# The moving operands of a four-layer encoder's products, moved to a pool with another byte offset

## The chip, the cores and the metric

The kernel runs on 1 core of one Trainium2 chip. The metric is the device time of one execution in microseconds (us), the median of the runs shown. Before the change it is 2073.7 us, the median of 3 runs (2072.6 to 2074.67).

## The reference

The input x has 256 tokens of 1024 features, in fp32. Four layers follow each other. Each is a gated feed-forward block (FFN), a mixer, and a second FFN, all with a residual connection and an RMS norm ahead of them:

```
for i in range(4):
    x = x + 0.5 * swiglu(rms_norm(x, norms[i, 0]), ffn_w_in[i, 0], ffn_w_out[i, 0])
    hn = rms_norm(x, norms[i, 1])
    y = (short_conv, hyena, gated_deltanet, short_conv)[i](hn)
    x = x + y
    x = x + 0.5 * swiglu(rms_norm(x, norms[i, 2]), ffn_w_in[i, 1], ffn_w_out[i, 1])
return rms_norm(x, final_norm)

def swiglu(x, w_in, w_out):          # w_in 1024 x 5632, w_out 2816 x 1024
    g, u = split(x @ w_in, 2)
    return (silu(g) * u) @ w_out
```

The short convolution projects x to 3 x 1024 features, multiplies two of the parts, convolves them over 3 tokens and gates and projects back. Hyena does the same with a long convolution by a Fourier transform, and the gated delta net is a linear attention with 8 heads. Nearly all arithmetic is in the products with the weights, some 350 MB of fp32 that are read once.

## The kernel before

**Layout of the work.** Activations lie with features on the partitions and the 256 tokens along the free axis; a tile of 128 features is 128x256. The weights are cut on the host into 665 *parts* of 128x1024 fp32, in the order in which they are used: a "c" part holds 128 output columns of a weight for all eight contraction tiles side by side, an "r" part holds 128 rows. A loop over phases (12 of them: FFN, mixer, FFN for each layer) asks for one part after the other.

**Split products.** TensorE takes the operands as float32r, and each fp32 operand is split into a high and a low half. `cut_part` (lines 263 to 285) does it for a weight part: ScalarE (ACT) copies `raw` to `wh` (L279), VectorE (DVE) subtracts to get `wl` (L281). `split_x` (L336) does it for the normalized x (`xh`, `xl`), `split` (L449) for the gated tiles that enter an output product (`hh`, `hl`). Every product of a 128x128 weight slice with a 128x256 activation tile is then three matmuls in `mm3` (L322 to L326): high weight by high activation (L324), low weight by high activation (L325), high weight by low activation (L326). The weight slice is the stationary operand, which an LDWEIGHTS puts into the array before each matmul (the profile shows it as PEld), and the activation tile is the moving operand, 256 columns of 4 bytes.

A part thus stands for 8 x 3 = 24 matmuls. In an FFN, `g` is the PSUM bank of the projection (moving operands `xh` and `xl`) and `accf` the four banks of the output product (moving operands `hh` and `hl`). `c`, `b` and `accs` are the same in the short convolution, `xv`, `x` and `acch` in hyena, `p` and `accd` in the gated delta net. In hyena `vf` and `vi` are the two halves of the Fourier transform, also by `mm3`: in `vf` a table (`th`, `tl`) is stationary and the turned values `vth`, `vtl` are moving, in `vi` the spectra `sh`, `sl` are stationary and a table is moving.

**Order.** The instructions of each engine run in the order in which the program issues them. SyncE (SP) issues the loads of `raw`, two parts (1 MB) each, into two buffers. `wh` and `wl` have rings of five parts, so the cuts on ACT and DVE run up to five parts ahead of TensorE.

**Where the tiles lie.** A pool of tiles takes a stretch of every partition; inside it each tag gets its buffers one behind the other in the order in which the tags first come up, in multiples of 32 bytes, and the pools stand one behind the other in the order in which they are opened. In the program before the change the byte addresses within a partition are:

```
pool  tile                                        first byte   byte mod 512
rp    raw, 2 buffers of 8192 bytes                     30976   256
rp    wh, 5 buffers of 4096 (wl: from 67840)           47360   256
tp    sq0, then xh0, xl0, ... xh3, xl3 (2048 each)     88320   256
tp    hh, 4 buffers of 1024                           119104   320
tp    hl, 4 buffers of 1024                           123200   320
hp    th, tl: the tables of the transform             130368   320
tq    vth, vtl; sh, sl (hyena)                        181824    64
tq    hh, hl of hyena's tiles 4 to 7                  204352    64
```

A weight slice of 128 columns is 512 bytes and an activation tile 1024 bytes, so every slice of a tile has the tile's offset modulo 512. `rp` ends at byte 88320.

In hyena the last tiles of the output product are split into the pool `tq`, since line 773 reads `self.split(y, f"{ng}_{f}", None if f < 4 else tp)` with `tp = self.tq`. The gated delta net borrows the buffers of `xh` and `xl` for its states and right sides (`xtile`), when x is no longer wanted.

Of the kernel before, what the change touches and what calls it, by code (L numbers as in the profile page):

```python
# [11 lines left out]
F32 = mybir.dt.float32  # L12
F32R = mybir.dt.float32r
# [23 lines left out]

PHASES = []
# [12 lines left out]
# ---------------------------------------------------------------- layouts  # L51
# Weight parts [128, 1024]: ("c", W, c0) = columns c0..c0+127 of W, all 8
# contraction tiles side by side; ("r", W, r0) = rows r0..r0+127 of W.
def out_tiles(f, n):
    """Rows of the output product that follow the projection of tile f."""
    if f <= LAG:
        return []
    lo = 0 if f == LAG + 1 else f - LAG
    return [t for t in range(lo, f - LAG + 1) if t < n - TAIL]
# [120 lines left out]
def shape_tables():  # L180
    f = np.float32
    # masks and ones
    i = np.arange(P)
    k, s = i[:, None], i[None, :]
    msk = np.concatenate([(k > s), (k <= s), (k < s), (k >= s), (k == s), np.ones((P, P))], axis=1).astype(f)
    # positional features of the filter network, transposed
    t = np.linspace(0.0, 1.0, L, dtype=f)[:, None]
    w = (f(2.0 * math.pi) * np.arange(L, dtype=f)[:, None] / f(L)).astype(f)
    fr = np.linspace(1e-4, 15, 16, dtype=f)[None, :]
    ph = (fr * w).astype(f)  # L190
    z = np.concatenate([t, np.cos(ph), -np.sin(ph)], axis=-1).astype(f)
    zt = np.zeros((P, L), f)
    zt[:33] = z.T
    lo, hi = math.log(1e-2) / 1.5, math.log(1e-2) / 0.3
    deltas = np.linspace(lo, hi, D, dtype=f)
    dec = np.exp((-t * np.abs(deltas)[None, :]).astype(f)).astype(f)
    dec = dec.reshape(2, P, D).transpose(1, 0, 2).reshape(P, 2 * D)
    # 512-point transform of 256 samples, frequencies 0..255 and, in place of
    # the zero sine, the Nyquist one
    n = np.arange(L)  # L200
    ang = 2.0 * math.pi * ((n[:, None] * n[None, :]) % 512) / 512.0
    fwd = np.concatenate([np.cos(ang), -np.sin(ang)], axis=1)
    fwd[:, L] = (-1.0) ** n
    inv = np.concatenate([2.0 * np.cos(ang), -2.0 * np.sin(ang)], axis=0) / 512.0
    inv[0] = 1.0 / 512.0
    inv[L] = (-1.0) ** n / 512.0
    fwd = fwd.reshape(2, P, 512).transpose(1, 0, 2).reshape(P, 1024)
    inv = inv.reshape(4, P, L).transpose(1, 0, 2).reshape(P, 1024)
    return np.concatenate([msk, zt], axis=1), dec, np.stack([fwd, inv]).astype(f)
# [5 lines left out]
# ---------------------------------------------------------------- program  # L215
class Prog:
    def __init__(self, nc, tc, io, phases, pools):
        self.nc, self.tc, self.io, self.phases = nc, tc, io, phases
        self.cp, self.rp, self.tp, self.ps = pools
        self.nparts = len(part_list(phases))  # L220
        self.next_part = 0
        self.raw = {}
        self.late = set()
        self.narrow = set()
        self.held = {}
        n = 0
        for ph in phases:
            if n:
                self.late |= {n + 3, n + 4}
            if ph[0] == "gd":  # L230
                self.narrow.add(n)
            n += len(part_list([ph]))
        self.bg = []
        self.ready = []

    # ---- weight stream
    def load_group(self, lo, n):
        nc = self.nc
        t = self.rp.tile([P, GRP, D], F32, name=f"raw{lo}", tag="raw", bufs=RAW)
        if lo < 5:  # L240
            # the first parts come in small pieces
            for o in range(n):
                step = 512 if lo + o < 3 else D
                for c in range(0, D, step):
                    self.load = nc.sync.dma_start(t[:, o, c:c + step], self.io["w"][lo + o, :, c:c + step])
        else:
            self.load = nc.sync.dma_start(t[:, :n, :], self.io["w"][lo:lo + n].rearrange("n p c -> p n c"))
# [3 lines left out]
    def load_behind(self, dst, src):  # L251
        """A load that keeps its place behind the weights."""
# [33 lines left out]
    def behind(self, i, z):  # L286
        """Parts that a new phase wants late are split behind the split of x."""
# [10 lines left out]
    # ---- products: out[col, tok] (+)= part' @ x  # L298
# [10 lines left out]
    def proj_first(self, outs):  # L309
        """A phase's first products: several parts side by side, so that the  # L310
        last tiles of x are wanted late. outs: (destination, start)."""
# [19 lines left out]
    # ---- residual update, split of x*g, and 1/rms  # L331
# [4 lines left out]
    def split_x(self, m, ng):  # L336
        nc = self.nc
        ph = self.tp.tile([P, 512], F32R, name=f"xh{ng}_{m}", tag=f"xh{m}", bufs=1)
        pl = self.tp.tile([P, 512], F32R, name=f"xl{ng}_{m}", tag=f"xl{m}", bufs=1)
# [21 lines left out]
    def rstd(self, ng, squared=False):  # L361
        """1/rms of the tokens, on every partition. Two stages, each to be
        issued behind other products."""
# [28 lines left out]
    # ---- accumulation of the output product  # L392
# [16 lines left out]
    def finish(self, pend, scale, bias, nxt):  # L409
        """The last output products, bank by bank, each bank's part of the  # L410
        residual stream updated as soon as it is complete."""
# [37 lines left out]
    def split(self, src, name, pool=None):  # L449
        """High and low parts of an SBUF tile."""  # L450
        pool = pool or self.tp
# [9 lines left out]
    # ---- phases  # L461
# [37 lines left out]
    def conv3(self, out, u, w, j, on_act=True):  # L499
        """out[t] = w0 u[t-1] + w1 u[t] + w2 u[t+1] along the free axis."""  # L500
# [50 lines left out]
    # ---- hyena: filters (spectra of the two-sided filter), then the mixer  # L551
    def sine(self, out, pre, bias, freq, tag):
        """out = sin(freq * (pre + bias)), the argument brought into [-pi, pi]."""
# [16 lines left out]
    def hy_setup(self):  # L570
        """Filter network up to its last layer; the rest goes to the background."""
# [42 lines left out]
        for c in range(2):  # L614
# [3 lines left out]
            def taps(b, c=c, cs=cs, eo=eo):  # L618
# [8 lines left out]
                if b == 0:  # L627
                    nc.vector.memset(hs[1][0:1, :], 0.0)
                    # v * d_bias is the filter's tap at zero
# [34 lines left out]
    def hy(self, ng, nxt):  # L664
# [6 lines left out]
        # constants of the short convolution: b_in enters through its taps  # L671
# [13 lines left out]
        def conv(pt, j, tag, bufs):  # L685
            """short convolution of one bank: columns j[0], j[1] of 128 features"""
# [28 lines left out]
        def turn(pr):  # L715
            """the pair's gated values with tokens on partitions"""
# [98 lines left out]
    # ---- gated delta rule, chunks of 128 tokens, both directions. With A the  # L815
    # strictly triangular matrix of a chunk, columns scaled by
    # gamma = beta / |k|^2, the chunk's solution is w = gamma * (I + A)^-1 r and
    # all products use the unscaled k and q.
    def gd(self, ng, nxt):
# [33 lines left out]
        # a large negative exponent outside the triangles  # L853
# [17 lines left out]
        def gates2(ab):  # L871
# [8 lines left out]
            # log(1 + exp(x)) = max(x, 0) + 2 atanh(u / (2 + u)), u = exp(-|x|)  # L880
# [28 lines left out]
        def decay(rg, hg, b, d):  # L909
            """E[s, c] = exp(sum of g over the tokens after s up to c), 0 outside the triangle"""  # L910
# [8 lines left out]
        def weights():  # L919
            """exp of the sums of g from a token to its chunk's end or start"""  # L920
# [17 lines left out]
        def turn(srcs, name):  # L938
            """[features, tokens] of two heads -> one bank [tokens, block, head, features]"""
# [45 lines left out]
        def kk(pr):  # L985
            """B = transposed -A of both directions"""
# [5 lines left out]
        def later():  # L992
            """Pool's work that nothing waits for yet"""
# [28 lines left out]
        # -- inverses of the 32 x 32 diagonal blocks, one block per partition  # L1022
        inv = {}

        def gather():
# [16 lines left out]
            # M[c, s] and the inverse's transpose X[s, c]; the two 16 x 16 blocks of the diagonal  # L1042
# [11 lines left out]
        def corner(stage, q):  # L1054
            """lower left 16 x 16 block: the second block's inverse times M21 times the first's"""
# [24 lines left out]
        # index 0 of the pair: block rows handled first by the recursion  # L1080
# [4 lines left out]
        def level64a(b):  # L1085
            """off-diagonal 32 x 32 blocks of the inverses of the 64 x 64 ones, and
            both put in the place of the matrix itself"""
# [38 lines left out]
        # -- chunks  # L1126
        w, S, Z, R2, wd, ot = {}, {}, {}, {}, {}, {}

        def xtile(tag, name):
            return self.tp.tile([P, 4, P], F32, name=name, tag=tag, bufs=1)  # L1130

        def solve_a(hg, b, rhs):
            """first half rows, and the right side as far as the diagonal blocks go"""
# [37 lines left out]
        def state(hg, tag):  # L1171
            """the states that the second chunks start from"""
# [11 lines left out]
        def carry(hg, tag):  # L1184
            """right sides of the second chunks"""
# [12 lines left out]
        def outp(hg, b):  # L1198
# [20 lines left out]
            # 1 / rms of o, which still lacks the factor 1 / |q| / sqrt(dk)  # L1219
# [17 lines left out]
        # -- order of work: after[n] is issued behind the products of part n  # L1237
# [23 lines left out]
        def late_silu(v):  # L1261
            """no change of table between the decays"""
# [15 lines left out]
        def unpack():  # L1278
            """convolution and silu of the heads whose bank is complete"""
# [96 lines left out]
    def final_piece(self, m):  # L1376
        """Sums of squares of a pair of feature tiles, and the pair times the
        norm's weight with tokens on partitions."""
# [54 lines left out]
    # ---- whole  # L1433
    def setup(self):
# [23 lines left out]
        # the engines' clock and table come up while the first loads run  # L1458
# [7 lines left out]
    def setup_rest(self):  # L1466
        """Tables and parameters that the first products do without."""
# [58 lines left out]
def build(nc, phases):  # L1526
# [17 lines left out]
    with tile.TileContext(nc) as tc:  # L1544
        with tc.tile_pool(name="cp", bufs=1) as cp, tc.tile_pool(name="rp", bufs=1) as rp, \
                tc.tile_pool(name="tp", bufs=1) as tp, \
                tc.tile_pool(name="ps", bufs=1, space=bass.MemoryType.PSUM) as ps:
            Prog(nc, tc, io, phases, (cp, rp, tp, ps)).run()
# [24 lines left out]
```

## Time and profile before

| what | before |
|---|---|
| time, median of 3 runs | 2073.7 us (2072.6 to 2074.67) |
| the profiled execution, first to last instruction (span) | 2073.3 us |
| TensorE (PE) busy, matmuls | 2048.9 us (99%), 17234 |
| weight loads (PEld) busy | 2028.2 us (98%), 17234 |
| VectorE (DVE) busy | 1407.5 us (68%) |
| ScalarE (ACT) busy | 1014.2 us (49%) |
| GpSimd (POOL) busy | 73.8 us (4%) |
| DMA | 356.76 MB, mean 172 GB/s |

The profile has no other time of that execution than the span; between it and the median of the runs lie 0.4 us. "Busy" counts a matmul from its start to its modelled end, and matmuls overlap in the pipeline: a matmul of 256 columns stands there with about 280 ns, while the next one starts some 120 ns after it. How fast TensorE works is therefore read from the distance of the starts, in the timeline, and not from the busy share. PEclk is the granted clock of TensorE, 1.00 being 2.4 GHz and 0.50 being 1.2 GHz.

### The profile page before, as it was taken

Reading aid. Unit: us, or ns where it says so; the run is one execution under the profiler, and the core shown is the slowest. Engines: PE = TensorE matmul, PEld = TensorE weight load, DVE = VectorE, ACT = ScalarE, POOL = GpSimd, SP = SyncE. Lnnn points to the kernel's source line nnn. Section 1 sums busy time; section 2 is a strip of 40 time slices with the busy share of each in tenths; the row PEclk is TensorE's granted clock in tenths of the full one; section 3 lists DMA queues with packets and bytes.
Section 4 is the critical chain, followed back from the end, with each engine's and each line's share of the span. In section 5 each row is a group of like instructions: output and inputs, shape, how many; then the busy total and the mean of one; then the engine's idle time right before and its main releaser. Section 6 shows DMA issues by size and latency. Waiting matters only on the chain.

```text
span 2073.3 us, 40294 instructions
## 1 busy us (share of the span) xinstructions
PE 2048.9 (99%) x17234; PEld 2028.2 (98%) x17234; DVE 1407.5 (68%) x2155; ACT 1014.2 (49%) x1546; POOL 73.8 (4%) x75
## 2 busy tenths in 40 slices
PE   9999999999999999999999998999999999999998
PEld 9999999999999999999999998899999999999998
DVE  6766867666666798666766689866667666767664
ACT  6444545445444555444544476555445444545443
POOL 0000000000000110000000021000000000000000
PEclk9999999999999999999999999999999999999999
DMA  7644455555555443555555532315554555555552
GB/s 249 233 164 153 153 183 183 183 183 173 194 183 184 163 158 128 196 184 187 181 184 185 185 123 102 123 62 185 184 184 169 199 185 185 179 185 181 186 186 95
DMA packets 93990, 356.76 MB, mean 172 GB/s; under 512 B 5810, under 2 KB 7218, under 8 KB 93619
## 3 DMA queue, kind: packets, MB, share of 16 engines
q1 hardware_dynamic: 93666, 354.18, 50.1%
q8 instruction: 135, 2.21, 0.4%
q14 instruction: 45, 0.36, 0.1%
q10 hardware_dynamic: 144, 0.00, 0.0%
HBM read 353.11 MB, written 1.05 MB: 171 GB/s over the span
## 4 chain that ended last, share of the span: by engine, by line
PE 89%; DVE 7%; DMA 2%; ACT 1%; issue 1%; POOL 0%; SPq 0%; POOLq 0%; DVEq 0%; ACTq 0%
PE g L324 16%; PE g L326 16%; PE g L325 16%; PE accf L324 8%; PE accf L326 8%; PE accf L325 8%; DVE wl L281 2%; PE c L324 1%; PE c L326 1%; PE c L325 1%; DMA raw<-w 1%; PE b L325 1%; PE b L324 1%; PE b L326 1%; PE accs L324 1%
## 5 line engine op out<-in xcount | busy, mean ns | idle before, releaser
L281 DVE TENSOR_TENSOR wl<-raw,wh 128x1024 fp32r<-128x1024 f32 (+1 forms) x667 | 811.2, 1221 | 430.7 <-ACT wh L279 430.3
L279 ACT ACTIVATE wh<-raw 128x1024 fp32r<-128x1024 f32 (+1 forms) x667 | 696.1, 1051 | 670.4 <-PE g L326 476.5
L324 PE MATMUL g<-xh,wh 128*128 128x256 f32 x2816 | 799.6, 284 | 1.0 <-ACT xh L344 0.7
L326 PE MATMUL g<-xl,wh 128*128 128x256 f32 x2816 | 798.3, 283 | 0.0
L325 PE MATMUL g<-xh,wl 128*128 128x256 f32 x2816 | 797.4, 283 | 0.3 <-DVE wl L281 0.3
L324 PEld LDWEIGHTS g<-xh,wh 128*128 128x128 f32 x2816 | 540.5, 192 | 4.1 <-ACT wh L279 2.8
L325 PEld LDWEIGHTS g<-xh,wl 128*128 128x128 f32 x2816 | 539.9, 192 | 0.6 <-DVE wl L281 0.5
L326 PEld LDWEIGHTS g<-xl,wh 128*128 128x128 f32 x2816 | 539.9, 192 | 0.2 <-DVE xl L345 0.2
L324 PE MATMUL accf<-hh,wh 128*128 128x256 f32 x1408 | 394.8, 280 | 0.0
L326 PE MATMUL accf<-hl,wh 128*128 128x256 f32 x1408 | 393.0, 279 | 0.0
L325 PE MATMUL accf<-hh,wl 128*128 128x256 f32 x1408 | 392.9, 279 | 0.0
L324 PEld LDWEIGHTS accf<-hh,wh 128*128 128x128 f32 x1408 | 264.9, 188 | 1.2 <-ACT hh L454 0.8
L326 PEld LDWEIGHTS accf<-hl,wh 128*128 128x128 f32 x1408 | 264.5, 188 | 0.0
L325 PEld LDWEIGHTS accf<-hh,wl 128*128 128x128 f32 x1408 | 264.2, 188 | 0.1
L454 ACT ACTIVATE hh<-t 128x256 fp32r<-128x256 f32 x192 | 79.8, 416 | 194.0 <-DVE t L474 189.7
L471 DVE TENSOR_TENSOR t<-g,rs 128x256 f32<-128x256 f32 x176 | 74.5, 423 | 83.8 <-PE g L326 77.2
L455 DVE TENSOR_TENSOR hl<-t,hh 128x256 fp32r<-128x256 f32 x192 | 81.4, 424 | 69.8 <-ACT hh L454 69.8
L325 PE MATMUL p<-xh,wl 128*128 128x256 f32 x256 | 74.5, 291 | 8.1 <-DVE wl L281 8.1
L472 ACT ACTIVATE t<-t 128x256 f32<-128x256 f32 x176 | 71.0, 404 | 23.4 <-DVE t L471 23.2
L324 PE MATMUL p<-xh,wh 128*128 128x256 f32 x256 | 75.8, 296 | 1.4 <-ACT wh L279 1.4
L474 DVE TENSOR_TENSOR t<-t,t 128x256 f32<-128x256 f32 x176 | 73.5, 418 | 1.5 <-ACT t L472 1.4
L326 PE MATMUL p<-xl,wh 128*128 128x256 f32 x256 | 74.1, 290 | 0.0
(315 smaller groups left out, 2424.7 us busy)
## 6 DMA issues: line engine op xcount, KB each, us to landing
raw<-w SPq DMA_DIRECT2D x330, 1024.0 KB, 4.8
raw<-w SPq DMA_DIRECT2D x6, 256.0 KB, 5.4
x<-x SPq DMA_DIRECT2D x4, 256.0 KB, 4.8
raw<-w SPq DMA_DIRECT2D x2, 512.0 KB, 6.1
dec<-dec SPq DMA_DIRECT2D x1, 1024.0 KB, 7.0
traw<-dft SPq DMA_DIRECT2D x2, 512.0 KB, 6.2
out<-ob SPq DMA_DIRECT2D x4, 256.0 KB, 2.4
w<-w SPq DMA_DIRECT2D x1, 512.0 KB, 9.0
```

The lines of the kernel that those rows point to most:

```text
L279: nc.scalar.activation(hi[:, s], src[:, s], AF.Copy)
L281: nc.vector.tensor_tensor(lo[:, s], src[:, s], hi[:, s].bitcast(F32), op=ALU.subtract)
L324: mm(out, ah, bh, start=start, stop=False, skip_group_check=True)
L325: mm(out, al, bh, start=False, stop=False, skip_group_check=True)
L326: mm(out, ah, bl, start=False, stop=stop, skip_group_check=True)
L454: self.nc.scalar.activation(hh, src, AF.Copy)
L455: self.nc.vector.tensor_tensor(hl, src, hh.bitcast(F32), op=ALU.subtract)
L471: nc.vector.tensor_tensor(t1, pg[f][:, :L], self.rs, op=ALU.mult)
L472: nc.scalar.activation(t1, t1, AF.Silu)
L474: nc.vector.tensor_tensor(t2, t1, t2, op=ALU.mult)
```

## The change

A new pool `mv` is opened between `rp` and `tp`. Its first tile, `lead`, has 80 words (320 bytes) and is never written. The tiles `xh`, `xl` (2048 bytes each, eight of them) and `hh`, `hl` (1024 bytes each, four of each) are taken from `mv` instead of `tp`; so are the gated delta net's borrowed tiles of these tags. By the rule above `mv` begins at byte 88320, `xh0` at 88640, which is byte 64 of 512, the first `hh` at 105024 (64 of 512), and `mv` ends at 113216, where `tp` begins. The rings `wh` and `wl` stay where they are, at 256 of 512. Everything opened after `tp` moves up by 320 bytes: hyena's own tiles go from 64 to 384 of 512 (`vth`, `vtl`, `sh`, `sl`, and `hh`, `hl` of its tiles 4 to 7), the transform's tables from 320 to 128. No instruction is added, removed or reordered. Comments were also dropped from the source.

```diff
+LEAD = 80
...
-        self.cp, self.rp, self.tp, self.ps = pools
+        self.cp, self.rp, self.mv, self.tp, self.ps = pools
...
+        self.mv.tile([P, LEAD], F32, name="lead")
...
-        ph = self.tp.tile([P, 512], F32R, name=f"xh{ng}_{m}", tag=f"xh{m}", bufs=1)
-        pl = self.tp.tile([P, 512], F32R, name=f"xl{ng}_{m}", tag=f"xl{m}", bufs=1)
+        ph = self.mv.tile([P, 512], F32R, name=f"xh{ng}_{m}", tag=f"xh{m}", bufs=1)
+        pl = self.mv.tile([P, 512], F32R, name=f"xl{ng}_{m}", tag=f"xl{m}", bufs=1)
...
-        pool = pool or self.tp
+        pool = pool or self.mv
         hh = pool.tile([P, L], F32R, name=f"hh{name}", tag="hh", bufs=4)
         hl = pool.tile([P, L], F32R, name=f"hl{name}", tag="hl", bufs=4)
...
         def xtile(tag, name):
-            return self.tp.tile([P, 4, P], F32, name=name, tag=tag, bufs=1)
+            pool = self.tp if tag.startswith("sq") else self.mv
+            return pool.tile([P, 4, P], F32, name=name, tag=tag, bufs=1)
...
         with tc.tile_pool(name="cp", bufs=1) as cp, tc.tile_pool(name="rp", bufs=1) as rp, \
-                tc.tile_pool(name="tp", bufs=1) as tp, \
+                tc.tile_pool(name="mv", bufs=1) as mv, tc.tile_pool(name="tp", bufs=1) as tp, \
                 tc.tile_pool(name="ps", bufs=1, space=bass.MemoryType.PSUM) as ps:
-            Prog(nc, tc, io, phases, (cp, rp, tp, ps)).run()
+            Prog(nc, tc, io, phases, (cp, rp, mv, tp, ps)).run()
```

## Rows read from the trace of the kernel before

**Rows 1.** The page: busy time by engine, and the chain that ended last.
```profile
PE 2048.9 (99%) x17234; PEld 2028.2 (98%) x17234; DVE 1407.5 (68%) x2155; ACT 1014.2 (49%) x1546; POOL 73.8 (4%) x75
...
PE 89%; DVE 7%; DMA 2%; ACT 1%; issue 1%; POOL 0%; SPq 0%; POOLq 0%; DVEq 0%; ACTq 0%
```
**Rows 2.** PE's groups: line, shapes, xcount | busy us, mean ns | idle before.
```profile
L324 PE MATMUL g<-xh,wh 128*128 128x256 f32 x2816 | 799.6, 284 | 1.0 <-ACT xh L344 0.7 <-ACT wh L279 0.3
...
L325 PE MATMUL accf<-hh,wl 128*128 128x256 f32 x1408 | 392.9, 279 | 0.0
...
L325 PE MATMUL p<-xh,wl 128*128 128x256 f32 x256 | 74.5, 291 | 8.1 <-DVE wl L281 8.1
...
L325 PE MATMUL c<-xh,wl 128*128 128x256 f32 x256 | 72.4, 283 | 0.0
...
L325 PE MATMUL xv<-xh,wl 128*128 128x256 f32 x128 | 36.3, 284 | 0.2 <-DVE wl L281 0.2
L325 PE MATMUL b<-xh,wl 128*128 128x256 f32 x128 | 36.2, 283 | 0.0
...
L325 PE MATMUL accs<-hh,wl 128*128 128x256 f32 x128 | 35.7, 279 | 0.0
```
**Rows 3.** Timeline of PE in an FFN: start us, us, line, out<-in.
```profile
401.56 0.28 PE L326 MATMUL accf<-hl,wh 128*128 128x256 f32 x1
...
404.15 0.29 PE L324 MATMUL g<-xh,wh 128*128 128x256 f32 x1
404.28 0.28 PE L325 MATMUL g<-xh,wl 128*128 128x256 f32 x1
...
405.00 0.28 PE L325 MATMUL g<-xh,wl 128*128 128x256 f32 x1
...
409.80 0.28 PE L326 MATMUL g<-xl,wh 128*128 128x256 f32 x1
```
**Rows 4.** The same view at hyena's output product: tile 0; tiles 2, 3; from tile 5.
```profile
780.86 0.28 PE L324 MATMUL acch<-hh,wh 128*128 128x256 f32 x1
...
783.22 0.28 PE L326 MATMUL acch<-hl,wh 128*128 128x256 f32 x1
...
791.43 0.28 PE L326 MATMUL vf<-vtl,th 128*128 128x256 f32 x1
...
791.79 0.28 PE L326 MATMUL vf<-vtl,th 128*128 128x256 f32 x1
791.91 0.28 PE L324 MATMUL acch<-hh,wh 128*128 128x256 f32 x1
...
797.35 0.28 PE L324 MATMUL acch<-hh,wh 128*128 128x256 f32 x1
...
802.83 0.28 PE L326 MATMUL vi<-tl,sh 128*128 128x256 f32 x1
802.95 0.28 PE L324 MATMUL acch<-hh,wh 128*128 128x256 f32 x1
...
807.71 0.28 PE L324 MATMUL acch<-hh,wh 128*128 128x256 f32 x1
```
**Rows 5.** Stretches: busy us (xcount) of PE, PEld, DVE, ACT, POOL; PEclk, DMA share, GB/s.
```profile
780.80:783.20 2.40, 2.40 (x22) 2.40 (x22) 2.40 (x6) 1.14 (x2) 0.00 (x0) 1.00 0.00 0
...
791.95:797.20 5.25, 5.25 (x49) 5.25 (x48) 5.11 (x9) 2.33 (x3) 0.00 (x0) 1.00 0.62 203
```
**Rows 6.** The same view over stages: two of FFNs and short convolutions, hyena, delta net, start.
```profile
36.00:690.00 654.00, 653.97 (x5363) 644.69 (x5362) 431.68 (x628) 309.80 (x424) 9.66 (x10) 1.00 0.54 183
...
690.00:812.00 122.00, 121.69 (x1026) 121.29 (x1025) 107.47 (x183) 63.26 (x96) 18.84 (x23) 1.00 0.43 146
1179.00:1400.00 221.00, 206.28 (x1945) 196.73 (x1944) 180.85 (x363) 133.86 (x323) 28.06 (x23) 0.95 0.31 109
0.00:36.00 36.00, 33.16 (x245) 32.35 (x246) 25.60 (x44) 24.13 (x39) 3.20 (x6) 0.95 0.73 253
```
**Rows 7.** The page: DVE's cut of a weight part, its busy time, mean and idle time.
```profile
L281 DVE TENSOR_TENSOR wl<-raw,wh 128x1024 fp32r<-128x1024 f32 (+1 forms) x667 | 811.2, 1221 | 430.7 <-ACT wh L279 430.3
```

## The prediction

> **What bounds the kernel now.** The order of reading is: the page's busy times and chain, then PE's groups, then the timeline of PE, then the loads of the other engines in the same stretches. The page says that PE is busy over 99% of the span and that 89% of the chain that ended last is PE, 7% DVE [rows 1]. The groups show almost no idle time ahead of the large products: 1.0 us before 2816 matmuls of `g`, none before `accf`; the only large one is 8.1 us ahead of `p` in the delta net [rows 2]. So the span is set by the distance between the starts of successive matmuls, and that is to be read in the timeline.
>
> There it has more than one value, although every one of these matmuls has the same form (128x128 by 128x256, granted clock 1.00, that is 2.4 GHz). In `g`, 40 steps from 405.00 to 409.80 take 4.80 us: 120.0 ns. In `accf`, 22 steps from 401.56 to 404.15 take 2.59 us: 117.7 ns [rows 3]. In `acch` the first tile has 20 steps in 2.36 us, 118.0 ns; the tiles 2 and 3 have 48 steps from 791.91 to 797.35, 5.44 us, 113.3 ns; from tile 5 on it is 42 steps in 4.76 us, again 113.3 ns [rows 4].
>
> What differs? Not what the other engines do: the slow 118.0 ns was seen with the DMA engines at a share of 0.00, the fast 113.3 ns with the DMA at 0.62, DVE busy in both [rows 5]. What differs is the byte offset of the moving operand against that of the weight slice which is loaded meanwhile, by the table of addresses. The weights are at 256 of 512 in all three. `g` moves tiles at 256, `accf` and the early `acch` tiles at 320, the last four `acch` tiles at 64. The offset 256 gives 120.0, 320 gives 118 in all FFNs, 64 gives 113.3. One thing spoils the table: tiles 2 and 3 of `acch` lie at 320 and still run at 113.3. They come directly behind `vf`, whose moving operand lies at 64 [rows 4]. I read it so: load and matmul run side by side in a cycle that repeats itself, an offset can hold more than one such cycle, and the work before decides which. At 320 two are seen, at 64 against 256 only the fast one. It was reached from `vi`, which ran at 120, as in the step from 802.83 to 802.95 [rows 4], and kept to the end.
>
> **The change part by part.** It removes and adds no instruction, wait or transfer, so nothing is moved past a queue. What it may alter is the step of PE.
>
> (1) `g`, `c` and `b`: 3 x 2816, 3 x 256 and 3 x 128 matmuls (each has three such rows, of which one is shown) [rows 2], together 9600. `c` and `b` have the same mean as `g`, 283 ns, and are put at its step. Their moving operand goes from 256 to 64, the pair of the fast `acch`. If they take its step, each saves 120.0 - 113.3 = 6.7 ns: 64.3 us.
>
> (2) `accf` and `accs`: 3 x 1408 and 3 x 128, together 4608 [rows 2], from 320 to 64: 117.7 - 113.3 = 4.4 ns each, 20.3 us. With (1) this is 84.6 us, and it lies on the path wholly: in the stretch of FFNs and short convolutions PE is busy 653.97 of 654.00 us [rows 6].
>
> (3) Hyena and the delta net: `xv` and `x` (576 matmuls), `p` (768), at 6.7 ns 9.0 us; `accd` and the first half of `acch` (192 and 96) at up to 4.4 ns, 1.0 us, as half of the 96 already run fast. But here DVE is busy 107.47 of 122 us and 180.85 of 221 us [rows 6], and PE waits 8.1 us for a cut in `p`. A faster PE arrives earlier at the same waits. Bounds: nothing and 10 us. I take 3, nearer to nothing, since the DVE share of 82 to 88% leaves little to shorten.
>
> (4) The tiles 4 to 7 of hyena's output product move from 64 to 384, since they stay in `tq`. They are 96 matmuls that run at 113.3 today. No row shows 384 against 256; the bounds are 113.3 and 120.0, so 0 to 0.6 us lost. I take 0.3. The transform moves with its tables by the same 320 bytes, its two operands keep their distance; `vf` and `vi` stay at their 120: nothing. The fp32 products of the delta net, some 480 matmuls of 128 columns or fewer, shift too: at most 6.7 ns each either way, 3 us; I take nothing, as no row tells of a sign.
>
> (5) What a faster PE meets. The weights must come faster by 120/113.3, at most 1.06. In the FFNs DVE goes from 431.68 of 654, 66%, to 70%, ACT from 47% to 50%, the DMA from 183 to 194 GB/s, where the first 36 us show 253 GB/s [rows 6]. So the steady supply holds. At each of the 11 borders between phases, the new x must be updated and split before new parts are cut, and there PE comes nearest to its supply. The bounds are nothing and one cut on DVE per border, 1.22 us [rows 7], 13 us in all. I take 2, near nothing, since today PE's wait on cuts is 0.3 us in 2816 matmuls of `g` [rows 2].
>
> (6) Stores of ACT and DVE to the new places: the edit costs nothing there as long as PE covers them, with a third of DVE's time idle in the FFNs [rows 6]; without that cover a longer split would show as PE waiting for `hh` or `hl`.
>
> The sum: 84.6 + 3 - 0.3 - 2 = 85.3 us less. The profiled execution has a span of 2073.3 us, so 1988.0; the median of the runs lies 0.4 us above that span, so 1988.4, and I say 1988. What is late next: still PE, at 113.3 ns a step.
>
> Its own range: at best 84.6 + 10 + 0, about 1979; at worst 84.6 + 0 - 0.6 - 13 = 71.0, and so 2003.
>
> **The rivals.** (A) The other cycle. Since 320 holds two cycles, 64 may hold the slow one too, and the borders, with transposes and sums between the products, may start it each time. Then `g`, `c`, `b` go only to 117.7, 9600 x 2.3 = 22 us, and `accf` stays: 2052 (with mixtures in between). For it: tile 0 of `acch`, directly behind transposes, ran at 118.0. Against it: that tile lay at 320, and no matmul with 64 against 256 ran slow.
>
> (B) The offset is not the cause. Tiles 2 and 3 speak for it: same offset as `accf`, other step. Then something else at the end of hyena set the step, `g` stays at 120.0 and the time at 2074. Against it: `g` and `accf` alternate in each FFN, and the step changes with them within a few matmuls, through 128 ns from 404.15 to 404.28, to an exact 120.0 [rows 3], under the same weights, clock and engines; operand tiles and destination bank are all that is exchanged. By the Trainium skill, "TensorE: Matmul & The Clock Gate", Part 2, TensorE has two SBUF read ports, one for the moving operand and one for weight loads, and loading the next weights takes no read bandwidth from the running matmul. By that rule offsets would not meet at all, and the sum would be nothing, the time of B. The two steps of 120.0 and 117.7 ns for one form do not sit well with it.
>
> (C) Slower. The mechanism: one offset for all also gives all one cycle, and it is the slow one of 120.0. Today `accf` and `accs` are better than `g`; they would lose 4608 x 2.3 = 10.6 us, and nothing is gained: 2084. It decides wherever 64 against 256 settles above 117.7 after a border. For it: byte 64 alone is no charm, for `vf` moves operands at 64 against tables at 320 and takes 120 ns (791.43 to 791.79, 3 steps) [rows 4]. Distances of 256 run at 120, like distance 0. Against it: the pair 64 and 256 itself.
>
> (D) The change does not do what it says: `lead` is never written, and if it took no room, `xh` and `hh` would both lie at 256 against 256, the pair of today's `g`. That has the price of C, 2084.
>
> **How the numbers follow.** Forecast 0.62; A, mixtures included, 0.18; B 0.09; C 0.09; D 0.02. A measurement here can tell about 0.2% (4 us) from no change. The forecast and A are faster, 0.80; B is within it, 0.09; C and D slower, 0.11. The forecast's own range is 1979 to 2003. The range reaches on to A, up to 2052, and then leaves out B, C and D, 0.20.
>
> **What would show it.** In the changed kernel's timeline `g` and `accf` must have the same step, 113.3 ns, 24 matmuls in 2.72 us, in every FFN, with no 128 ns at the switch between them. PE's busy mean for `g` must fall below the 279 ns of today's `accf`, and a full 50 us of an FFN must hold some 441 matmuls. DVE's and ACT's busy times must stay, their shares rise. In (3) the idle time of PE before `p` must grow. Steps of 117.7 would show A; 120.0 in `g` with 117.7 in `accf` B; 120.0 in both C or D. The prediction is wrong if the mean step of `g` is over 115 ns, or if PE loses over 13 us waiting for cuts at the borders.

## The result and the profile after

The changed kernel takes 2016.5 us, the median of 4 runs (2012.1 to 2021.5), against 2074.2 (2072.6 to 2078.7, 4 runs) for the kernel before, run beside it: a ratio of 0.972, interval 0.9703 to 0.9736. The forecast was 1988, its range 1979 to 2052. The kernel is faster by 58 us where 85 were forecast.

The profiled execution has a span of 2013.4 us and a time of 2015.3. Its page answers to [rows 1, 2, 7] as follows: busy time by engine, the chain that ended last, then groups of instructions (line numbers are three higher than before).

```profile
PE 1986.9 (99%) x17234; PEld 1966.1 (98%) x17234; DVE 1405.1 (70%) x2155; ACT 1015.0 (50%) x1546; POOL 74.0 (4%) x75
...
PE 87%; DVE 7%; DMA 2%; ACT 2%; issue 1%; POOL 0%; SPq 0%; POOLq 0%; DVEq 0%; ACTq 0%
...
L284 DVE TENSOR_TENSOR wl<-raw,wh 128x1024 fp32r<-128x1024 f32 (+1 forms) x667 | 810.8, 1221 | 396.6 <-ACT wh L282 396.1
...
L327 PE MATMUL g<-xh,wh 128*128 128x256 f32 x2816 | 783.7, 278 | 0.1
...
L328 PE MATMUL accf<-hh,wl 128*128 128x256 f32 x1408 | 390.4, 277 | 0.0
...
L328 PE MATMUL p<-xh,wl 128*128 128x256 f32 x256 | 73.5, 288 | 8.8 <-DVE wl L284 8.8
```

The same counts, the same work on DVE and ACT, the same chain: only PE's busy time fell, by 62 us. `g`'s mean went from 284 to 278 ns and `accf`'s from 279 to 277. That is a mean distance of starts of 115.1 and 115.0 ns (all steps of these groups under 160 ns), which no stretch shows for long. The windows show two kinds of stretches instead. First the changed kernel, then the kernel before over the same microseconds; the columns are those of [rows 5].

```profile
236.00:500.00 264.00, 263.76 (x2222) 262.77 (x2221) 174.56 (x253) 125.76 (x172) 4.09 (x7) 1.00 0.54 187
511.00:686.00 175.00, 175.00 (x1546) 175.00 (x1546) 117.07 (x166) 87.07 (x121) 1.40 (x1) 1.00 0.56 193
```
```profile
236.00:500.00 264.00, 263.97 (x2191) 262.78 (x2190) 171.50 (x249) 123.00 (x166) 3.49 (x6) 1.00 0.54 184
511.00:686.00 175.00, 175.00 (x1469) 175.00 (x1469) 108.30 (x150) 79.41 (x106) 1.56 (x1) 1.00 0.55 187
```

From 511 to 686 us PE is never idle and starts a matmul every 175.00/1546 = 113.2 ns, against 119.1 before. From 236 to 500 it starts hardly more than before, and the timeline there has an exact 117.8. Two places near the beginning of an FFN, where TensorE itself computes something for the norm: sums (`pst`) in the FFN behind the short convolution, after which the step stays as it was, and two small products (`pbc`) in the next FFN, after which it is better (start, duration, line, out<-in):

```profile
319.20 0.28 PE L329 MATMUL g<-xl,wh 128*128 128x256 f32 x1
319.32 0.50 PE L373 MATMUL pst<-msk,sq 128*128 128x1 f32 x4
319.68 0.36 PE L327 MATMUL g<-xh,wh 128*128 128x256 f32 x1
319.88 0.28 PE L328 MATMUL g<-xh,wl 128*128 128x256 f32 x1
320.00 0.28 PE L329 MATMUL g<-xl,wh 128*128 128x256 f32 x1
320.12 0.28 PE L327 MATMUL g<-xh,wh 128*128 128x256 f32 x1
...
509.09 0.28 PE L329 MATMUL g<-xl,wh 128*128 128x256 f32 x1
...
510.15 0.28 PE L329 MATMUL g<-xl,wh 128*128 128x256 f32 x1
510.27 0.38 PE L383 MATMUL pbc<-msk,r 128*128 128x128 f32 x2
510.40 0.36 PE L327 MATMUL g<-xh,wh 128*128 128x256 f32 x1
510.60 0.28 PE L328 MATMUL g<-xh,wl 128*128 128x256 f32 x1
...
511.17 0.28 PE L327 MATMUL g<-xh,wh 128*128 128x256 f32 x1
```

From 509.09 to 510.15 nine steps take 1.06 us, 117.8 ns. Two small products (`pbc`) stand between, and from 510.60 to 511.17 five steps take 0.57 us, 114 ns by these rounded starts and 113.3 over the 175 us that follow. Behind the sums at 319.32 (`pst`) the step stays at 118. Tiles, weights' offset, clock and engines are the same on either side: one offset, two cycles, that is, two patterns of distances that repeat, one with a mean of 113.3 ns and one with 117.8. A disturbance can change the cycle. Without one it stays: 28 stretches have more than 30 large matmuls in a row with nothing between them, 13931 matmuls together, and behind its first dozen each of them keeps either 113.3 or 117.8 to its end. Of the 14208 large matmuls of FFNs and short convolutions 59% started within 115 ns of the one before and 40% between 115 and 119.5.

The lengths of the stages, from the first large matmul of each to that of the next, in us (the last two columns are experiments, below):

| stage | before | changed | changed, again | k_d112 |
|---|---|---|---|---|
| FFN, layer 0 first | 209.8 | 207.7 | 203.4 | 201.1 |
| short convolution | 99.2 | 97.7 | 97.7 | 95.2 |
| FFN, layer 0 second | 189.9 | 187.7 | 187.7 | 181.3 |
| FFN, layer 1 first | 189.7 | 180.6 | 180.6 | 180.2 |
| hyena | 117.1 | 115.9 | 116.0 | 115.4 |
| FFN, layer 1 second | 190.1 | 187.2 | 187.2 | 180.7 |
| FFN, layer 2 first | 190.4 | 181.3 | 181.3 | 181.0 |
| delta net | 206.2 | 206.4 | 205.4 | 204.4 |
| FFN, layer 2 second | 189.7 | 180.6 | 180.6 | 180.4 |
| FFN, layer 3 first | 189.7 | 180.3 | 180.3 | 180.2 |
| short convolution | 92.4 | 87.8 | 87.8 | 87.8 |
| FFN, layer 3 second, to the end | 203.8 | 194.7 | 201.2 | 194.8 |

Where the short cycle holds, a whole FFN gains 9 us, and where the other holds, 2 to 3.

### The profile page after: what moved, and what is told of

It is laid out like the page before. It is cut to its first block, busy times and chain, and to the rows that moved or that the text cites. A ratio compares the mean times of both kernels' runs of the same rounds, so it can differ in the third digit from the quotient of the medians.

```text
span 2013.4 us, 40294 instructions
## 1 busy us (share of the span) xinstructions
PE 1986.9 (99%) x17234; PEld 1966.1 (98%) x17234; DVE 1405.1 (70%) x2155; ACT 1015.0 (50%) x1546; POOL 74.0 (4%) x75
## 4 chain that ended last, share of the span: by engine, by line
PE 87%; DVE 7%; DMA 2%; ACT 2%; issue 1%; POOL 0%; SPq 0%; POOLq 0%; DVEq 0%; ACTq 0%
PE g L329 16%; PE g L328 16%; PE g L327 16%; PE accf L329 8%; PE accf L328 8%; PE accf L327 8%; DVE wl L284 2%; DMA raw<-w 2%; PE c L328 1%; PE c L327 1%; PE c L329 1%; PE accs L328 1%; PE b L328 1%; PE accs L327 1%; PE b L327 1%
## 5 line engine op out<-in xcount | busy, mean ns | idle before, releaser
L327 PE MATMUL g<-xh,wh 128*128 128x256 f32 x2816 | 783.7, 278 | 0.1
L329 PE MATMUL g<-xl,wh 128*128 128x256 f32 x2816 | 782.4, 278 | 0.0
L328 PE MATMUL g<-xh,wl 128*128 128x256 f32 x2816 | 782.2, 278 | 0.1
L327 PEld LDWEIGHTS g<-xh,wh 128*128 128x128 f32 x2816 | 529.3, 188 | 3.1 <-ACT wh L282 2.7
L328 PEld LDWEIGHTS g<-xh,wl 128*128 128x128 f32 x2816 | 529.8, 188 | 0.5 <-DVE wl L284 0.4
L329 PEld LDWEIGHTS g<-xl,wh 128*128 128x128 f32 x2816 | 529.2, 188 | 0.0
L327 PE MATMUL accf<-hh,wh 128*128 128x256 f32 x1408 | 390.4, 277 | 0.0
```

What stands on the lines that cost most here:

```text
L327: mm(out, ah, bh, start=start, stop=False, skip_group_check=True)
L328: mm(out, al, bh, start=False, stop=False, skip_group_check=True)
L329: mm(out, ah, bl, start=False, stop=stop, skip_group_check=True)
```

## The experiments

**Matmuls alone (m1_offsets).** No other engine works; one disturbance (two one-column sums, which the profile counts as four matmuls, or two transposes), then 48 matmuls (`LEN`) in the kernel's order of operands, and so on through the offsets. In `run` the last two numbers are the byte of the weights and that of the moving tile. It computes nothing of the reference.

```diff
+for rep in range(2):
+    for e in ("sum", "turn"):
+        for mv in range(0, 512, 32):
+            entry(e, f"A{rep}{e}{mv}")
+            run(f"A{rep}{e}{mv}", LEN, 256, mv)
+for e in ("sum", "turn"):
+    for st in range(0, 512, 64):
+        entry(e, f"B{e}{st}")
+        run(f"B{e}{st}", LEN, st, 64)
```

> A kernel of matmuls alone: runs of 48 in the pattern of the changed kernel (high weight by high activation, low by high, high by low; 128x128 by 128x256, float32r) with no other engine at work and no load of weights; it computes nothing of the reference. Part A keeps the weights at byte 256 of 512 and puts the moving operand at 0, 32, ... 480; each run comes once behind two 1-column sums and once behind two 128-column transposes, all of it twice. Part B keeps the moving operand at 64 and puts the weights at 0, 64, ... 448. Theory (the offset of the moving operand against the weights' sets which steps are possible, the work ahead picks one of them): 256 against 256 steps by 120.0 ns behind either; 64 and 320 against 256 step by 113.3 or 117.7 ns; in part B the steps follow the difference, so weights at 64 (difference 0) give 120.0 with the moving operand at 64. Rival 1 (accesses of DVE, ACT and the DMA to the same memory cost the 4 to 7 ns): all runs step by 113.3 ns or less, whatever the offset. Rival 2 (the place of the moving operand alone counts): part B steps by 113.3 or 117.7 ns throughout.

The timeline (start, duration, line, out<-in): behind sums, weights at 256, moving tiles at 0, at 64 and at 192 of 512; then moving tiles kept at 64 and weights at 64, 128 and 256 (`Bsum`), and at 384 behind transposes (`Bturn`). Each run ends where the next disturbance begins.

```profile
30.82 6.00 PE L52 MATMUL A0sum<-big 128*128 128x256 f32 x48
36.66 0.50 PE L59 MATMUL A0sum_e<-idn,one 128*128 128x1 f32 x4
...
43.08 5.90 PE L52 MATMUL A0sum<-big 128*128 128x256 f32 x48
48.82 0.50 PE L59 MATMUL A0sum_e<-idn,one 128*128 128x1 f32 x4
...
67.66 5.71 PE L52 MATMUL A0sum<-big 128*128 128x256 f32 x48
73.21 0.50 PE L59 MATMUL A0sum_e<-idn,one 128*128 128x1 f32 x4
...
420.33 6.00 PE L52 MATMUL Bsum<-big 128*128 128x256 f32 x48
426.18 0.50 PE L59 MATMUL Bsum_e<-idn,one 128*128 128x1 f32 x4
426.54 5.70 PE L52 MATMUL Bsum<-big 128*128 128x256 f32 x48
...
438.57 5.69 PE L52 MATMUL Bsum<-big 128*128 128x256 f32 x48
...
497.79 5.90 PE L52 MATMUL Bturn<-big 128*128 128x256 f32 x48
503.53 0.38 PE L62 MATMUL Bturn_e<-idn,one 128*128 128x128 f32 x2
```

The first run takes 36.66 - 30.82 = 5.84 us; its first step, behind the sums, is 0.20, and so the other 47 are 5.64/47 = 120.0 ns. Likewise 117.9 at 64, and 113.8 at 192, where the steps after the first eight are 113.33. Over all runs with the weights at 256, after the first eight steps: 0 gives 120.0, 32 gives 116.7, 64 gives 117.8, 96 gives 119.9 to 120.1, 128 gives 118.7, 160 gives 117.4 or 118.6, 192 gives 113.33, 224 gives 118.4, and every value repeats 256 bytes further. With the moving tile kept at 64 the weights alone change it: 120.0 at 64 and 320, 113.33 at 128. So the step hangs on the difference of the two offsets, modulo 256, and needs no other engine. And at 64 against 256 it was 117.8 in eight of eight runs, but in `Bsum` (438.57) 113.33: the forecast's one cycle for this pair fell here. The difference 192 has both cycles too: with weights at 384 it gave 113.33 behind sums and 117.8 behind transposes (497.79).

**Another difference in the kernel (k_lead48).** All of `xh`, `xl`, `hh`, `hl` at 448 of 512, a difference of 192. The matmuls alone gave 113.33 there in eight of eight runs with the weights at 256. The four runs of the same difference with the weights elsewhere were left out of that count, and one of them, the one at 497.79 above, had 117.8.

```diff
-LEAD = 80
+LEAD = 48
```

> The changed kernel with a lead of 48 words in place of 80, so that all moving operands lie at byte 448 of 512, 192 ahead of the weights modulo 256. Theory (the difference of moving operand and weights modulo 256 sets the possible steps; 64 has two, 117.8 and 113.3 ns, and 192 was at 113.3 ns in 8 of 8 runs of the kernel of matmuls alone): g and accf step by 113.3 ns in every FFN, and the time is the forecast's sum again, 1988 us (1980 to 1996). Rival (two steps are there at any difference, and the borders of phases pick one at random): stretches at 117.8 ns as in the changed kernel, 2005 to 2022 us.

Measured 2023.0 us (2020.0 to 2024.6), ratio 0.9757 (0.9744 to 0.9771): a miss. The mean step of `g` is 115.3 ns, and the mixture is there again, with the stages partly exchanged. The FFN from 511 us on, which ran at 113.2 in the changed kernel, now has the slow step, 175.00/1489 = 117.5:

```profile
236.00:500.00 264.00, 263.75 (x2283) 262.85 (x2282) 180.03 (x263) 129.27 (x178) 6.44 (x8) 1.00 0.55 187
511.00:686.00 175.00, 175.00 (x1489) 175.00 (x1489) 112.06 (x154) 82.24 (x112) 2.94 (x2) 1.00 0.54 184
```

That a difference gave one step behind two kinds of beginnings doesn't show that it has only one, and the first run had already shown both.

**The pool without its lead (k_nolead).** Everything at 256.

```diff
-        self.mv.tile([P, LEAD], F32, name="lead")
```

> The changed kernel without the lead tile: the pool is there, but xh, xl, hh, hl all lie at byte 256 of 512, the weights' own offset. Theory: g stays at 120.0 ns, and accf and accs, today's 117.7 ns, go to 120.0 too: 4608 matmuls by 2.3 ns, 10.6 us slower than before, 2084 us (2080 to 2088). Rival (the pool as such, the order of the tiles or what lies beside them, made the gain): 2012 to 2022 us as the whole change.

Measured 2083.5 us (2082.8 to 2086.1), ratio 1.0051 (1.0037 to 1.0065). `g` and `accf` both step at 120.0; their groups now have one mean, and `accf`'s 279 of [rows 2] is gone:

```profile
L327 PE MATMUL g<-xh,wl 128*128 128x256 f32 x2816 | 797.9, 283 | 0.1
...
L327 PE MATMUL accf<-hh,wl 128*128 128x256 f32 x1408 | 398.4, 283 | 0.0
```

The pool as such gives nothing, the price that the prediction put on D (2084) is met, and the whole gain is the lead's.

**Only `xh` and `xl` at 64 (k_xonly).** A second pad puts `hh` and `hl` back to 320 of 512.

```diff
+        if not hasattr(self, "pad"):
+            self.pad = self.mv.tile([P, 64], F32, name="pad")
         hh = pool.tile([P, L], F32R, name=f"hh{name}", tag="hh", bufs=4)
```

> The changed kernel with 256 bytes of padding ahead of hh and hl: xh and xl at byte 64 of 512, hh and hl at 320 as before the change. Theory (only the difference modulo 256 counts, and 64 and 320 are one and the same): the step of g is 113.3 or 117.8 ns by phase, and accf takes over the step of the g beside it, also 113.3 ns; time as with the whole change, 2010 to 2024 us. Rival (the step belongs to each offset modulo 512, and hh at 320 is the 117.7 ns of before): accf at 117.7 ns in all phases, some 12 us more, 2024 to 2036 us.

Measured 2018.5 us (2014.0 to 2019.8), ratio 0.9731 (0.9718 to 0.9745), as the changed kernel. `accf`, not moved, now steps at 115.4 on average and at 113.3 in the good stages. It had 117.7 at the same 320 before: there it always began right behind a `g` that ran at 120.0. What `accf` gained came from `g`, not from its own new place.

**A finer scan and more beginnings (m2_fine).** Offsets in steps of 16 and of 4 bytes, then ten kinds of beginnings (two or three sums or transposes, other products, waits for DVE).

```diff
+for mv in range(0, 256, 16):
...
+for mv in range(176, 212, 4):
...
+for e in (("sum", 2), ("sum", 3), ("turn", 2), ("turn", 3), ("run", 0), ("run", 96), ("run", 32),
+          ("wait", 1), ("wait", 2), ("wait", 3)):
+    for mv in (64, 192, 320, 448):
```

> Matmuls alone again, nothing of the reference is computed. Part A: moving operand at 0, 16, ... 240 against weights at 256, behind sums and behind transposes. Part B: at 176 to 208 in steps of 4 bytes. Part C: at 64, 192, 320 and 448, each behind ten different beginnings (two or three pairs of sums, of transposes, 24 matmuls at another offset, a wait for DVE). Theory: at 192 and 448 113.3 ns behind nearly all of the beginnings, at 64 and 320 either 113.3 or 117.8 ns; the odd offsets between 113.3 and 120.0 ns and none under 111 ns. Rival (the step is picked by the beginning alone): 192 and 448 have as many slow runs as 64 and 320.

At 64 two of ten beginnings led to 113.33 and eight to 117.8; at 320 three of ten; at 192 seven and at 448 six. Both differences have two cycles. That is fewer than the "nearly all" expected at 192 and 448, and more than at 64 and 320. The kind of the beginning doesn't settle it either: at 192, behind two transposes each time, the scan in steps of 16 bytes gave 117.8 and the one in steps of 4 gave 113.33. One offset of the scan stood out, 112, with 113.3 behind sums and behind transposes:

```profile
120.72 0.38 PE L62 MATMUL Aturn_e<-idn,one 128*128 128x128 f32 x2
120.86 5.72 PE L52 MATMUL Aturn<-big 128*128 128x256 f32 x48
126.41 0.50 PE L59 MATMUL Asum_e<-idn,one 128*128 128x1 f32 x4
126.78 5.95 PE L52 MATMUL Asum<-big 128*128 128x256 f32 x48
132.56 0.38 PE L62 MATMUL Aturn_e<-idn,one 128*128 128x128 f32 x2
```

The run at 112 takes 5.55 us, the next one, at 128, takes 5.78. The 4-byte steps, one run each, show no smooth law: 184 gives 120.0, 188 gives 115.5, 192 gives 113.3, 196 gives 120.1.

**112 against 64, and offsets that differ among the operands (m3_mixed).** Six beginnings at 16, 112, 64, 192; then 64 combinations in which `wl` and `xl` are shifted against `wh` and `xh`.

```diff
+for mv in (16, 112, 64, 192):
+    for e in (("sum", 1), ("sum", 3), ("turn", 1), ("turn", 3), ("run", 0), ("wait", 2)):
...
+for mv in range(0, 256, 64):
+    for dw in range(0, 256, 64):
+        for dx in range(0, 256, 64):
```

> Matmuls alone, nothing of the reference is computed; runs of 36. Part A: moving operand 16, 112, 64 and 192 bytes beyond the weights (modulo 256), each behind six beginnings. Part B: xh at 0, 64, 128, 192 against wh, with wl moved by 0, 64, 128, 192 bytes and xl by 0, 64, 128, 192 bytes of their own, 64 combinations, each behind sums and behind transposes. Theory (the differences of each matmul's moving operand and of the weights loaded beside it set the possible steps, the beginning picks one): 64 and 192 have fast runs (113.3 ns) and slow ones (117.8 ns), 192 more fast ones than 64; 0 in all places gives 120.0 ns; mixed differences give means between 113 and 121 ns, and a few hold the fast step behind both beginnings. Rival (only xh against wh counts): the steps don't change with the offsets of wl and xl.

At 64, behind one pair of transposes and behind three:

```profile
104.19 4.49 PE L52 MATMUL Aturn1x<-big 128*128 128x256 f32 x36
108.51 0.82 PE L62 MATMUL Aturn3x_e<-idn,one 128*128 128x128 f32 x6
109.08 4.33 PE L52 MATMUL Aturn3x<-big 128*128 128x256 f32 x36
113.25 1.00 PE L52 MATMUL Arun0x_r<-big 128*128 128x256 f32 x7
```

The same 36 matmuls take 4.32 us in one and 4.17 in the other. The counts of 113.3: at 16 two of six, at 64 one, at 192 three, at 112 six of six. The shifted combinations gave means between 113.4 and 122.3, where 121 was expected as the upper end. So the low halves count as well: with `xh` at the offset of `wh`, 120.0 became 115.6 when `wl` was moved by 64 and `xl` by 128 bytes, behind sums and behind transposes alike.

**The kernel at 112, and its control at 64 (k_d112, k_d64).** Tiles begin at multiples of 32 bytes, and 112 is none. So all of `xh` and `xl` become slices of one tile with a lead of 28 words (368 of 512), and all of `hh` and `hl` slices of another with 60 (112 of 512). The control has leads of 80 and 0 words instead, which is 64 of 512 for both.

```diff
-LEAD = 80
+LEAD = 28
+LEADH = 60
...
+        if m == 0:
+            self.xall = self.mv.tile([P, LEAD + 8 * 512], F32R, name=f"xall{ng}", tag="xall", bufs=1)
+        ph, pl = self.xslot(self.xall, "h", m), self.xslot(self.xall, "l", m)
...
+                self.hall = self.mv.tile([P, LEADH + 8 * L], F32R, name="hall")
+            o = LEADH + (self.nsplit % 4) * L
+            self.nsplit += 1
+            hh, hl = self.hall[:, o:o + L], self.hall[:, o + 4 * L:o + 5 * L]
```

> The same products in the same order, but the moving tiles lie so that their byte difference from the weight slices is 112 modulo 256 (xh, xl at 368 of 512, hh, hl at 112 of 512, weights at 256 as before), held in one tile for all of xh and xl and one for all of hh and hl. Theory (the difference alone fixes which cycles exist, and at 112 the one of 113.3 ns came from every beginning tried, 8 of 8 and 6 of 6 with matmuls alone): g, accf, c and accs step at 113.3 ns in every phase, no stretch at 117 or more outside the delta net's own products and hyena's tiles 4 to 7, busy mean of g below 277 ns; 59 us less than the changed kernel's profiled 2015.3 minus what is left of slow stretches (14208 matmuls at a mean excess of 1.75 ns = 25 us): 1988 us, range 1982 to 1997. Rival (any difference has a second, slower cycle that some border starts; 112 was lucky in the few beginnings): stretches at 118 to 119 ns in some phases, 2000 to 2022. Second rival (one tile for many operands adds waits among splits and products): idle time of PE before g or accf of several us at borders, step 113.3 all the same.

> The control for k_d112: the same joined tiles, but the lead chosen so that every moving tile is at byte 64 of 512 (difference 64 modulo 256), as in the changed kernel. Theory: the two cycles of 113.3 and 117.7 ns by phase, mean of g 115 ns or so, 2008 to 2024 us, as the changed kernel. Rival (joining the tiles is what changes the time): it goes with k_d112 and not with the changed kernel.

At 112, which the two kernels of matmuls alone had tried behind eight beginnings in all: 1991.8 us (1989.8 to 1993.5, 5 runs), ratio 0.9604 (0.9591 to 0.9617). The control: 2016.9 (2015.3 to 2019.0), ratio 0.9724 (0.9711 to 0.9738), as the changed kernel. The page of the kernel at 112:

```profile
PE 1957.7 (98%) x17234; PEld 1935.4 (97%) x17234; DVE 1404.2 (71%) x2155; ACT 1014.3 (51%) x1546; POOL 71.4 (4%) x75
...
L330 PE MATMUL g<-xall,wl 128*128 128x256 f32 x2816 | 776.0, 276 | 0.1
...
L330 PE MATMUL accf<-hall,wl 128*128 128x256 f32 x1408 | 387.3, 275 | 0.0
...
L330 PE MATMUL p<-xall,wl 128*128 128x256 f32 x256 | 72.5, 283 | 9.5 <-DVE wl L286 9.4
```

The stretch that the changed kernel spent at 117.8, in the kernel at 112 and then in the control:

```profile
236.00:500.00 264.00, 263.13 (x2302) 262.17 (x2301) 182.86 (x269) 133.00 (x184) 6.46 (x8) 1.00 0.56 190
```
```profile
236.00:500.00 264.00, 263.76 (x2224) 262.80 (x2223) 175.44 (x258) 126.81 (x175) 4.90 (x7) 1.00 0.54 183
```

At 112, 97.6% of the 14208 large matmuls start within 115 ns; the mean step is 113.45 ns. Most of the rest stand behind disturbances: there the step is 116 to 121 for up to 14 matmuls, and then the short cycle comes by itself. The trace has the counter-proof inside: hyena's tiles 4 to 7, left in `tq`, lie at 448 here, a difference of 192. Behind `vi` they keep 117.8 for all of the last three parts, and the `g` that follows without a disturbance, at 112, falls to 113 within a few matmuls:

```profile
776.82 0.28 PE L331 MATMUL acch<-hl,wh 128*128 128x256 f32 x1
...
778.59 0.28 PE L331 MATMUL acch<-hl,wh 128*128 128x256 f32 x1
778.71 0.28 PE L329 MATMUL g<-xall,wh 128*128 128x256 f32 x1
...
779.54 0.28 PE L330 MATMUL g<-xall,wl 128*128 128x256 f32 x1
...
781.12 0.28 PE L329 MATMUL g<-xall,wh 128*128 128x256 f32 x1
```

Fifteen steps to 778.59 take 1.77 us, fourteen from 779.54 take 1.58. The expected busy mean "below 277" and the 1988 us (1982 to 1997) were met, and the second rival's waits are absent: PE idles 0.1 us before this row of `g` and not at all before that of `accf`. It beats both kernels, and the control, which differs from it only in where the tiles lie, doesn't follow it.

**The changed kernel once more (k_again).** Unaltered, one run.

> The changed kernel once more, one look. Theory (at difference 64 the cycle is chosen anew at each disturbance by timing of some ns): the phases that run at 113.3 and those at 117.7 ns are partly others than in the first profile (there fast in the second FFN of layers 2 and 3 and in all of layer 4 bar borders, slow in the first two FFNs and hyena), time within 2005 to 2025 us. Rival (the cycle is fixed by the program's order): the same phases to the microsecond.

2016.3 us, and the table above shows its stages: ten of twelve have the length of the first profile within 1.1 us. Two differ, the first FFN (203.4 against 207.7) and the last (201.2 against 194.7). So neither expectation holds alone. The traces of k_xonly and k_d64, with the same order and the same difference of 64, say the same: all stages but the first FFN, the delta net and the last FFN agree in the four kernels within 0.2 us, and the last FFN takes 201.2 in three of them and 194.7 in one. In most places the program's order fixes the cycle, and in some it comes out either way. What tips it in those was not tried apart; the spread of the changed kernel's times (2012 to 2022, against 2072.6 to 2078.7 before) fits such changes of whole stages, which is argued and not shown.

## Why the prediction was right or wrong

The direction and the range held. The forecast's own range (1979 to 2003) did not: the rival A came true, in the mixtures that it was given. The time lies in the range only because the range reached on to A; the course held likeliest, at 0.62, did not come.

**The step that failed** is the reading "At 320 two are seen, at 64 against 256 only the fast one." The 42 steps of [rows 4] were one run behind one beginning. Since only the difference modulo 256 counts, 320 and 64 against 256 are the same pair, so the table of addresses already held the counter-example: `accf` in [rows 3] and tile 0 in [rows 4] ran at 117.7 and 118.0. The prediction argued against A that this "tile lay at 320", which was no argument. In the changed kernel 40% of the large matmuls took the long cycle, and that kept 25.6 of the 84.6 us.

**(1) and (2)** were priced rightly and paid in part. The 14208 large matmuls stood above 113.33 ns by 84.9 us together before (84.6 forecast), by 25.6 us after, and by 1.7 us at 112. The change took 59.3 of it; the span fell by 59.9. The kernel at 112 took 83.2, with a span of 1987.9. So the mechanism and its size were right, and the offset was not the one that secures it.

**(3)** Hyena and the delta net gave 1.2 us and took 0.2: 1.0 in all, with the loss of (4) in it, within the bounds of 0 and 10, below the 3 taken. PE's wait in `p` grew from 8.1 to 8.8 us, as foretold.

**(4)** Hyena's tiles 4 to 7, now at 384 against 256, step at 118.6, where the matmuls alone gave 118.7 for a difference of 128. That costs 96 x 5.3 = 0.5 us, where 0.3 was taken and 0.6 was the bound.

**(5)** The borders cost nearly nothing. Steps above 160 ns, waits and disturbances together, exceed 113.3 by 7.4 us before and 7.7 after, 0.3 more where 2 was taken; at 112 it is 8.5. **(6)** DVE and ACT keep their busy times within 3 us.

**The signs.** Of those that the prediction named, the equal step of `g` and `accf`, the missing 128 ns at the switch, the mean of `g` below 279 and 441 matmuls in 50 us (1546 in 175) came; the last one only in some stages. The mean step of `g`, 115.1, stands just past the 115 set as the limit.

**B, C and D** fell: the step does follow the offsets with nothing else at work, `g` fell from 120.0, and `lead` takes its room. By the Trainium skill, "TensorE: Matmul & The Clock Gate", Part 2, loading the next weights doesn't take read bandwidth from the running matmul, since each has its own port. For the time of a stream the runs here do not bear that out: the same 48 matmuls took 5.84 us or 5.55, by where the weights and the moving operand lay against each other. Whether read bandwidth is what the slower ones lack, no run shows.

## What to carry to other kernels

Where matmuls stand back to back with a weight load each, read the distance of the starts, not the busy share; if it isn't the same everywhere, compare the byte offsets of the two operands. Before an offset is called good, try it behind many different beginnings: a repeating cycle can keep whatever its beginning gave it, and a single long stretch counts as one sample. Of two offsets with the same best step, the one that returns to it by itself is worth more (here 25 us of 2016).

## What the runs showed of the hardware

- One form of matmul at a granted clock of 1.00 has mean steps between 113.3 and 120.1 ns when all moving tiles share an offset, by the difference of moving operand and weights modulo 256 bytes; with offsets that differ among the tiles, up to 122.3.
- It needs no other engine: matmuls alone showed 120.0, 117.8 and 113.3, the steps of [rows 3, 4].
- At 64 and 192 two cycles last (113.3 and 117.8), at 0 only 120.0 was seen to last, and at 112 only 113.3, behind every beginning tried, and in the kernel after at most 14 matmuls.
- Four bytes can decide: 113.3 or 117.8 at 192, and 120.1 at 196, the last from a single run.

Why these differences and not others is open; no run here looks into the cycle itself.
